# Strassen pairs of projections in the dilated part of an attention layer

## The chip, the cores and the metric

The kernel runs on one core of one Trainium2 chip, as one program. The metric is the device time of an execution in microseconds (us); lower is better. Times of before are the median of three runs, and a profile was taken of one more execution.

## The reference

The reference is an encoder trunk with two layers on 512 tokens of width 1024: h += Mixer(RMSNorm(h)), then h += SwiGLU(RMSNorm(h)). Layer 0 mixes by dilated sliding-window attention in three groups of 16 heads of 64, layer 1 by gated linear attention. The change lies in the first mixer:

```python
qkv = (h @ w_in).reshape(bsz, seq, A_N_GROUPS, 3, A_HEADS, A_HEAD_DIM)
for g, (window, dilation) in enumerate(((128, 1), (512, 4), (2048, 16))):
    q = rope(rms_norm(qkv[:, :, g, 0], q_gain[g]), positions)
    k = rope(rms_norm(qkv[:, :, g, 1], k_gain[g]), positions)
    v = qkv[:, :, g, 2]
    o, lse = dilated_window_attention(q, k, v, window, dilation)
...
alpha = softmax(stack(lses), axis=0)
out = sum(alpha[..., None] * stack(outs), axis=0)
return out.reshape(bsz, seq, A_WIDTH) @ w_out
```

## The kernel before

Everything is float32. A matrix product is made of three on TensorE (PE): both operands are split into a high and a low part, and hi·hi, hi·lo and lo·hi are added up in PSUM. A weight tile of 128 x 1024 comes by a DMA of 512 KB on the SP queue (`weight`), `split` copies it to the high part on ScalarE (ACT, L96) and subtracts that on VectorE (DVE, L97). There are two buffers for what is loaded (`wf`) and three each for the parts (`wh`, `wl`). The names in the profile are these tags: `wl<-wf,wh` is a low part being made.

The order of the instructions on each engine is laid down when the program is built, by a scheduler that goes by the order of the code and by priorities: loading and splitting stand under `high_priority(offset=AHEAD)` with AHEAD = 100, so they are drawn ahead of other work by so many places. Each engine then works through its own list strictly in order, waiting where an operand or a buffer isn't there.

The stages are: dilated attention (groups with dilations 4 and 16 together, 0 to about 414 us), local attention (to about 560), the output projection, the first FFN, the linear attention (about 950 to 1130), and the second FFN. The dilated part runs in four rounds u = 0 to 3 of four heads of either group. `attend_dilated` (L706) makes for each u a k chunk, a v chunk and a q chunk, and then attention. A chunk (`chunk_of`, L534) is a plain product of 512 tokens and 1024 features with 512 columns: 8 feature tiles x 4 token tiles x 3 = 96 matmuls of 128x512 (L548 to L550), four `pp` accumulators in PSUM (all that there are) and 4 weight tiles, each of which feeds 24 matmuls. Local attention begins with a chunk of the same size for its own q and k.

Behind a k or q chunk `qk_chunk` (L559) normalises and rotates: of each of four 128x512 tiles ACT copies the accumulator and squares it, DVE sums the squares by head (L573, L574), finds the reciprocal root (L116 to L119), multiplies by the tables of cosines and sines (L587, and in halves L588 and L589), adds (L590) and scales (L592). Then PE transposes in 16 blocks (L597) and the results are copied by ACT and DVE (L604, L606). All four tiles must be done before the first transpose. Attention computes scores on PE, softmax on DVE and ACT (L627, L628), transposes (L640), weighs v (L680), transposes back (L698) and stores by POOL's DMA queue (L719, L747).

The FFN's `gate_up` already uses seven products in place of eight, after Strassen: the inputs are cut into halves by features and tokens, the weights into halves by features and by the two columns that belong together, and sums of these are multiplied (`forms` L237 for weights, `product` L318 with L329 to L331). A product is 4 feature tiles x 2 token tiles x 3 = 24 matmuls and takes two split weight tiles, each feeding 12. Weight sums are made there by adding DMAs on POOL's queue (L252), 512 KB each, or on DVE.

The lines that the change and the prediction touch are in the functions below.

## Time and profile before

| | |
|---|---|
| time, median of three runs | 1509.53 us (1508.55 to 1509.82) |
| profiled execution, its own time | 1508.64 us |
| its span | 1506.8 us |
| PE busy | 1491.7 us, 99%, 8142 instructions |
| DVE busy | 947.9 us, 63% |
| ACT busy | 781.8 us, 52% |
| POOL busy | 110.3 us, 7% |
| HBM traffic | 121 GB/s over the span |

PE is the matrix engine; PEld, its weight loads, overlaps it. Busy time is the time in which an engine has an instruction running; consecutive instructions overlap, so a step is better read from start to start in a timeline. A row of a timeline has start and duration in us, the engine, the line in the kernel, the operation, out<-in by tile names without their numbers, and the shapes; brackets tell how long the engine had been idle before it and what ended that. A row of waits tells which instruction of which engine waited for what, and the total in us, the number and the longest. The row of a group has its instruction count, its busy time in us and the mean in ns, then the idle time in front of it.

### The profile page before, as it was taken

Reading aid. Unit: us, or ns where it says so; the run is one execution under the profiler, and the core shown is the slowest. Engines: PE = TensorE matmul, PEld = TensorE weight load, DVE = VectorE, ACT = ScalarE, POOL = GpSimd, SP = SyncE. Lnnn points to the kernel's source line nnn. Section 1 sums busy time; section 2 is a strip of 40 time slices with the busy share of each in tenths; the row PEclk is TensorE's granted clock in tenths of the full one; section 3 lists DMA queues with packets and bytes.
Section 4 is the critical chain, followed back from the end, with each engine's and each line's share of the span. In section 5 each row is a group of like instructions: output and inputs, shape, how many; then the busy total and the mean of one; then the engine's idle time right before and its main releaser. Section 6 shows DMA issues by size and latency. Waiting matters only on the chain.

```text
span 1506.8 us, 21145 instructions
## 1 busy us (share of the span) xinstructions
PE 1491.7 (99%) x8142; PEld 1225.9 (81%) x8142; DVE 947.9 (63%) x1728; ACT 781.8 (52%) x1348; POOL 110.3 (7%) x192
## 2 busy tenths in 40 slices
PE   8999999999999999999999999999999999999998
PEld 6878787887877878888888887888888888888887
DVE  6584766777476778866667334837476866668222
ACT  6353453545466655755567233545644855568121
POOL 0001010101010010211110000000010211110000
PEclk9999999999999999999999999999999999999999
DMA  8423222243222136777674333212156676675331
GB/s 281 158 67 94 81 79 84 85 128 99 74 71 71 44 121 194 224 168 156 148 162 129 92 100 96 91 56 78 46 157 188 195 170 153 156 152 147 118 110 60
DMA packets 59829, 183.95 MB, mean 122 GB/s; under 512 B 10032, under 2 KB 10608, under 8 KB 59728
## 3 DMA queue, kind: packets, MB, share of 16 engines
q1 hardware_dynamic: 44912, 133.17, 27.0%
q0 software_dynamic: 14816, 49.42, 16.4%
q8 instruction: 64, 1.05, 0.3%
q14 instruction: 37, 0.30, 0.1%
HBM read 174.11 MB, written 8.46 MB: 121 GB/s over the span
## 4 chain that ended last, share of the span: by engine, by line
PE 87%; DVE 8%; ACT 2%; DMA 1%; issue 1%; SPq 0%; ACTq 0%; DVEq 0%
PE ppp L109 9%; PE ppp L108 9%; PE ppp L110 9%; PE ppp L549 8%; PE ppp L550 8%; PE ppp L548 8%; PE ppp L329 6%; PE ppp L330 6%; PE ppp L331 6%; PE ps L331 2%; PE ps L329 2%; PE ps L330 2%; PE po L680 2%; PE ps L640 1%; DVE wl L97 1%
## 5 line engine op out<-in xcount | busy, mean ns | idle before, releaser
L97 DVE TENSOR_TENSOR wl<-wf,wh 128x1024 fp32r<-128x1024 f32 (+1 forms) x184 | 220.6, 1200 | 229.8 <-ACT wh L96 229.0
L96 ACT ACTIVATE wh<-wf 128x1024 fp32r<-128x1024 f32 (+1 forms) x184 | 191.3, 1040 | 326.7 <-PE ppp L109 195.2
L548 PE MATMUL ppp<-wh,xs 128*128 128x512 f32 (+1 forms) x672 | 256.7, 386 | 5.5 <-ACT wh L96 5.5
L549 PE MATMUL ppp<-wl,xs 128*128 128x512 f32 (+1 forms) x672 | 257.7, 383 | 0.7 <-DVE wl L97 0.3
L550 PE MATMUL ppp<-wh,xs 128*128 128x512 f32 (+1 forms) x672 | 257.5, 383 | 0.0
L548 PEld LDWEIGHTS ppp<-wh,xs 128*128 128x128 f32 x672 | 126.6, 189 | 32.4 <-ACT wh L96 5.5
L549 PEld LDWEIGHTS ppp<-wl,xs 128*128 128x128 f32 x672 | 126.8, 189 | 26.5 <-DVE wl L97 2.9
L550 PEld LDWEIGHTS ppp<-wh,xs 128*128 128x128 f32 x672 | 126.8, 189 | 25.0 <-issue 1.3
L97 DVE TENSOR_TENSOR wl<-wA,wh 128x1024 fp32r<-128x1024 f32 x88 | 107.6, 1222 | 37.8 <-ACT wh L96 37.8
L96 ACT ACTIVATE wh<-wA 128x1024 fp32r<-128x1024 f32 x88 | 93.2, 1059 | 62.1 <-PE ppp L331 45.8
L329 PE MATMUL ppp<-wh,a 128*128 128x512 f32 (+1 forms) x288 | 108.1, 381 | 0.0
L108 PE MATMUL ppp<-xs,wh 128*128 128x512 f32 x272 | 107.4, 396 | 0.0
L330 PE MATMUL ppp<-wl,a 128*128 128x512 f32 (+1 forms) x288 | 107.4, 373 | 0.0
L331 PE MATMUL ppp<-wh,a 128*128 128x512 f32 (+1 forms) x288 | 107.3, 374 | 0.0
L109 PE MATMUL ppp<-xs,wh 128*128 128x512 f32 x272 | 106.6, 393 | 0.0
L110 PE MATMUL ppp<-xs,wl 128*128 128x512 f32 x272 | 106.0, 391 | 0.0
L97 DVE TENSOR_TENSOR wl<-wB,wh 128x1024 fp32r<-128x1024 f32 x38 | 46.5, 1225 | 73.7 <-ACT wh L96 73.7
L628 ACT ACTIVATE sm<-sm,st 128x160 f32<-128x160 f32 (+2 forms) x128 | 56.8, 447 | 40.9 <-DVE st L627 40.8
L329 PE MATMUL ps<-wh,sh 128*128 128x512 f32 (+1 forms) x192 | 73.1, 381 | 0.0
L329 PE MATMUL ppp<-wh,sh 128*128 128x512 f32 (+1 forms) x192 | 72.2, 376 | 0.0
L331 PE MATMUL ppp<-wh,sl 128*128 128x512 f32 (+1 forms) x192 | 71.6, 373 | 0.0
L331 PE MATMUL ps<-wh,sl 128*128 128x512 f32 (+1 forms) x192 | 71.5, 373 | 0.0
(319 smaller groups left out, 2955.0 us busy)
## 6 DMA issues: line engine op xcount, KB each, us to landing
wA<-in_gate_up_dram POOLq DMA_DIRECT2D x52, 512.0 KB, 5.5
wf<-in_down_dram SPq DMA_DIRECT2D x32, 512.0 KB, 3.5
wf<-in_gate_up_dram SPq DMA_DIRECT2D x24, 512.0 KB, 4.5
wf<-in_a_w_v_dram SPq DMA_DIRECT2D x20, 512.0 KB, 3.4
wB<-in_gate_up_dram POOLq DMA_DIRECT2D x20, 512.0 KB, 5.5
wf<-in_a_w_q_dram SPq DMA_DIRECT2D x16, 512.0 KB, 3.3
wf<-in_a_w_qk_dram SPq DMA_DIRECT2D x16, 512.0 KB, 3.3
wB<-in_gate_up_dram SPq DMA_DIRECT2D x16, 512.0 KB, 3.3
```

Source lines behind the costliest of these rows:

```text
L96: nc.scalar.activation(hi, src, AF.Copy)
L97: self.low = nc.vector.tensor_sub(lo, src, hi.bitcast(F32))
L108: mm(out, lhsT=wh, rhs=xh, start=start, stop=False)
L109: mm(out, lhsT=wh, rhs=xl, start=False, stop=False)
L110: self.multiplied = mm(out, lhsT=wl, rhs=xh, start=False, stop=stop)
L329: mm(a, lhsT=xh[:, tok], rhs=wh[:, f], start=start and k == 0, stop=False, skip_group_check=True)
L330: mm(a, lhsT=xh[:, tok], rhs=wl[:, f], start=False, stop=False, skip_group_check=True)
L331: self.multiplied = mm(a, lhsT=xl[:, tok], rhs=wh[:, f], start=False, stop=k == last, skip_group_check=True)
L548: mm(a, lhsT=xh, rhs=wh[:, f], start=k == 0, stop=False)
L549: mm(a, lhsT=xh, rhs=wl[:, f], start=False, stop=False)
L550: self.multiplied = mm(a, lhsT=xl, rhs=wh[:, f], start=False, stop=k == KT - 1)
L628: nc.scalar.activation(sm[:, w], sm[:, w], AF.Exp, bias=n, scale=-1.0, accum_out=l)
```

## The change

The first k and the first q chunk stay plain. The other ten projections of the dilated part are made in five pairs, in this order: (v0,v1), (k1,q1), (k2,q2), (v2,v3), (k3,q3). A pair is one seven-product multiplication of halves: four halves of the input (by features and tokens), two projections side by side, 7 x 24 = 168 matmuls instead of 2 x 96 = 192.

- `input_sums` makes the four sums S1 to S4 of the input's halves, once, from the same rows that the plain chunk of k0 used. They lie in slots of the residual `h` and of other tiles that are free in this stage (`xs`, `h`, `R`, `acc`, `sq`, `fa`).
- `pair_forms` makes the seven forms of the weights: 8 plain loads on SP and 8 adding ones on POOL's queue, 512 KB each. Forms 3 and 5 are made in the tiles of forms 2 and 4: they are added to once those have been split. 14 tiles are split for a pair, instead of 8 for two chunks.
- `pair` multiplies in the order A11, S1, S2, S4, S3, A12, A22, on two pairs of `pp` accumulators in turn, and puts the results together: copies on ACT, four operations on DVE that read PSUM and add, and two additions. The second projection's four tiles are complete after the fifth product, the first one's after the seventh.
- The rotation is a function of its own, `rotated`, called first for q (the second of a pair) and then for k. Four small operations for the mean square are joined in one.
- Slots: `qk` 16 instead of 20, one of `qtmp` and `t2` instead of two; the tables for local attention are made at its start.

In after.py `split` is at L97 (ACT) and L98 (DVE), the plain chunk at L551 to L553, `product` at L330 to L332, and the operations of `rotated` at L585 to L616.

```diff
     BASE = {"xs": 16, "h": 8, "wf": 2, "wh": 3, "wl": 3, "R": 1, "acc": 1, "sq": 1,
             "cols": 1, "ident": 1, "ones": 1, "eps": 1}
-    ATTN = {"qk": 20, "v": 8, "zs": 4, "wa": 4, "wb": 2, "sm": 3, "pt": 4, "ob": 2, "on": 2, "ao": 4,
-            "tab": 2, "masks": 1, "ms": 1, "Rc": 1, "ebias": 1, "mst": 1,
-            "qv": 2, "qr": 2, "qtmp": 2, "st": 2, "t2": 2, "stn": 2, "st0": 2, "mw": 2, "mL": 5}
+    LOCAL = {"ao": 4, "on": 2, "tab": 2}
+    DILATED = {"zx": 4, "wA": 2, "wB": 2, "fa": 1}
+    ATTN = {"qk": 16, "v": 8, "zs": 4, "wa": 4, "wb": 2, "sm": 3, "pt": 4, "ob": 2, "masks": 1, "mRc": 1, "ms": 1, "Rc": 1, "ebias": 1, "mst": 1,
+            "qv": 2, "qr": 2, "qtmp": 1, "st": 2, "t2": 1, "stn": 2, "st0": 2, "mw": 2, "mL": 5}
...
+        self.tables({"k": ((1, 1), (1, 2)), "q": ((0, 1), (0, 2))}, 0, "pt", "qk")
...
+        return self.rotated(kind, rc, copy)
+
+    def rotated(self, kind, rc, source):
+        nc = self.nc
         zs = []
         v = self.t("qv", (P, 4, 8))
         for i in range(NT):
-            z = self.t("zs")
-            nc.scalar.activation(z, acc[i], AF.Copy)
+            z = source(i)
             sq = self.t("wb")
             nc.scalar.activation(sq, z, AF.Square)
             nc.vector.tensor_reduce(v[:, i], sq.rearrange("p (h d) -> p h d", d=HD), AX.X, ALU.add)
-            nc.vector.tensor_scalar(v[:, i], v[:, i], 1.0 / HD, self.ebias[:, rc + i:rc + i + 1],
-                                    op0=ALU.mult, op1=ALU.add)
             zs.append(z)
+        nc.vector.scalar_tensor_tensor(v, v, 1.0 / HD, self.ebias[:, rc:rc + 4].unsqueeze(2).to_broadcast([P, 4, 8]),
+                                       op0=ALU.mult, op1=ALU.add)
...
+    def split_tokens(self, k, i):
+        tok = slice(i % 2 * P, (i % 2 + 1) * P)
+        return [x[:, tok] for x in self.x[k][i // 2]]
+
+    def input_sums(self):
+        nc = self.nc
+        stt = nc.vector.scalar_tensor_tensor
+        half = KT // 2
+        minus = self.t("mst", (P, 4))
+        nc.vector.tensor_scalar(minus, self.cols[:, half:KT], -1.0, None, op0=ALU.mult)
+        tags = iter(["xs"] * 4 + ["h"] * 8 + ["R", "acc", "sq", "fa"])
+        out = []
+        for m in range(half):
+            lo = [self.t(next(tags), (P, 2, 256), F32R) for _ in range(2)]
+            hi = [self.t(next(tags), (P, 2, 256), F32R) for _ in range(2)]
+            raw = [self.t(tag, (P, 2, 256)) for tag in ("pt", "sm")]
+            f = [raw[i // 2][:, i % 2] for i in range(4)]
+            upper, lower = self.raw[m], self.raw[half + m]
+            nc.scalar.activation(raw[1], upper.rearrange("p (a b) -> p a b", b=256), AF.Copy,
+                                 scale=self.cols[:, m:m + 1])
+            stt(f[0], lower[:, 256:S], self.cols[:, half + m:half + m + 1], f[3], op0=ALU.mult, op1=ALU.subtract)
+            stt(f[1], f[0], -1.0, f[2], op0=ALU.mult, op1=ALU.subtract)
+            nc.vector.tensor_sub(f[2], f[2], f[3])
+            stt(f[3], lower[:, 0:256], minus[:, m:m + 1], f[1], op0=ALU.mult, op1=ALU.subtract)
+            for i in range(2):
+                nc.scalar.activation(hi[i], raw[i], AF.Copy)
+                nc.vector.tensor_sub(lo[i], raw[i], hi[i].bitcast(F32))
+            out.append([(hi[i // 2][:, i % 2], lo[i // 2][:, i % 2]) for i in range(4)])
+        self.raw = None
+        x = self.x
+        self.forms_of_x = [[x[m][0] for m in range(half)], [x[half + m][0] for m in range(half)],
+                           [x[half + m][1] for m in range(half)]] + [[out[m][i] for m in range(half)] for i in range(4)]
+
+    def pair_forms(self, first, second):
+        def load(tag, dram):
+            tiles = []
+            for i in range(2):
+                w = self.t(tag, (P, 1024))
+                self.nc.sync.dma_start(w, dram[i])
+                tiles.append(w)
+            return tiles
+
+        def add(tiles, dram):
+            for i in range(2):
+                self.nc.gpsimd.dma_start(tiles[i], dram[i], accum_op=ALU.add)
+
+        def ready(tiles):
+            return [self.split(w, (P, 1024), "wh", "wl") for w in tiles]
+
+        def steps():
+            a = load("wA", first[0:2])
+            add(a, second[0:2])
+            yield ready(load("wf", first[0:2]))
+            b = load("wB", second[2:4])
+            w = ready(a)
+            add(a, second[2:4])
+            yield w
+            yield ready(a)
+            add(a, first[2:4])
+            w = ready(b)
+            add(b, second[0:2])
+            yield w
+            yield ready(b)
+            yield ready(load("wf", first[2:4]))
+            yield ready(a)
+
+        gen = steps()
+        for _ in range(7):
+            with self.tc.high_priority(offset=AHEAD):
+                w = next(gen)
+            yield w
+
+    def pair(self, first, second, tile_of, scale):
+        nc = self.nc
+        A11, A12, A22, S1, S2, S3, S4 = self.forms_of_x
+        w = self.pair_forms(first, second)
+        b1 = [self.p("pp") for _ in range(2)]
+        b3 = [self.p("pp") for _ in range(2)]
+        out = [[None] * NT for _ in range(2)]
+
+        def copy(dst, src, c, i):
+            nc.scalar.activation(dst, src, AF.Copy, scale=scale(c, i))
+            return dst
+
+        self.product(b1, A11, next(w), S, True)
+        for i in range(2):
+            out[0][i] = copy(tile_of(0, i), b1[i], 0, i)
+        self.product(b3, S1, next(w), S, True)
+        for i in range(2):
+            out[1][2 + i] = copy(tile_of(1, 2 + i), b3[i], 1, 2 + i)
+        self.product(b1, S2, next(w), S, False)
+        for i in range(2):
+            out[1][i] = copy(tile_of(1, i), b1[i], 1, i)
+        self.product(b3, S4, next(w), S, False)
+        for i in range(2):
+            e = out[1][i]
+            nc.vector.scalar_tensor_tensor(e, b3[i], scale(1, i), e, op0=ALU.mult, op1=ALU.add)
+        self.product(b1, S3, next(w), S, False)
+        for i in range(2):
+            e = out[1][2 + i]
+            t = copy(self.t("zs"), b1[i], 1, 2 + i)
+            nc.vector.tensor_add(e, e, t)
+        yield out[1]
+        self.product(b3, A12, next(w), S, True)
+        for i in range(2):
+            e = out[0][i]
+            nc.vector.scalar_tensor_tensor(e, b3[i], scale(0, i), e, op0=ALU.mult, op1=ALU.add)
+        self.product(b1, A22, next(w), S, False)
+        for i in range(2):
+            out[0][2 + i] = copy(tile_of(0, 2 + i), b1[i], 0, 2 + i)
+        yield out[0]
+
+    def qk_pair(self, u):
+        early = lambda c, i: self.t("zx" if (c == 0) == (i < 2) else "zs")
+        sums = self.pair(self.ins["a_w_k"][u], self.ins["a_w_q"][u], early, lambda c, i: (1.0, -1.0)[c])
+        z = next(sums)
+        q = self.rotated("q", 0, lambda i: z[i])
+        z = next(sums)
+        k = self.rotated("k", 0, lambda i: z[i])
+        return k, q
+
+    def v_pair(self, u):
+        scale = lambda c, i: (self.Rc, self.minus_Rc)[c][:, i:i + 1]
+        sums = self.pair(self.ins["a_w_v"][u], self.ins["a_w_v"][u + 1], lambda c, i: self.t("v"), scale)
+        second, first = next(sums), next(sums)
+        return first, second
 
     def attention(self):
         self.masks = None
         self.pending = None
         self.later = []
         with self.phase("attn", self.ATTN):
-            self.ready = self.first_tiles()
-            far = [self.attend_dilated(u) for u in range(4)]
+            far = []
+            with self.phase("dilated", self.DILATED):
+                self.ready = self.first_tiles()
+                k = self.qk_chunk("k", 0)
+                self.input_sums()
+                q = self.qk_chunk("q", 0)
+                v = self.v_pair(0)
+                far.append(self.attend_dilated(0, k, v[0], q))
+                k, q = self.qk_pair(1)
+                far.append(self.attend_dilated(1, k, v[1], q))
+                k, q = self.qk_pair(2)
+                v = self.v_pair(2)
+                far.append(self.attend_dilated(2, k, v[0], q))
+                k, q = self.qk_pair(3)
+                far.append(self.attend_dilated(3, k, v[1], q))
+                self.forms_of_x = None
```

How this moves instructions. First PE, at the end of u=1's last projection (q in before; k and q together now). `wh` and `wl` are a weight tile's parts, `xs` the input's, `ppp` the accumulators, `wa` a rotated tile. Before:

```order
L548 MATMUL ppp_1377<-wh_1470,xs_166 128x512
L549 MATMUL ppp_1377<-wl_1471,xs_166 128x512
L550 MATMUL ppp_1377<-wh_1470,xs_167 128x512
L548 MATMUL ppp_1847<-wh_1853,xs_82 128x512
L549 MATMUL ppp_1847<-wl_1854,xs_82 128x512
L550 MATMUL ppp_1847<-wh_1853,xs_83 128x512
...
L549 MATMUL ppp_1847<-wl_1914,xs_142 128x512
L550 MATMUL ppp_1847<-wh_1913,xs_143 128x512
L597 MATMUL ps_1559<-ident_65,wa_1552 128x128
```

After:

```order
L330 MATMUL ppp_1237<-wh_1560,xs_177 128x512
L331 MATMUL ppp_1237<-wl_1561,xs_177 128x512
L332 MATMUL ppp_1237<-wh_1560,xs_178 128x512
L330 MATMUL ppp_1930<-wh_1944,xs_85 128x512
L330 MATMUL ppp_1931<-wh_1944,xs_85 128x512
L330 MATMUL ppp_1932<-wh_1984,xs_452 128x512
L330 MATMUL ppp_1933<-wh_1984,xs_452 128x512
L609 MATMUL ps_1490<-ident_65,wa_1483 128x128
...
L331 MATMUL ppp_1930<-wl_1945,xs_85 128x512
L330 MATMUL ppp_1930<-wh_1944,xs_99 128x512
L609 MATMUL ps_1642<-ident_65,wa_1635 128x128
```

Before, 63 matmuls of the next chunk stand between the last one of the projection and the first transpose of q (`wa_1552`). Now it is 4 matmuls to the first transpose of q (`wa_1483`), then q's 16 transposes, then 5 more matmuls to the first of k (`wa_1635`); the first of those five reads `wl_1945`, and the others stand behind it.

Now DVE at the same place; `wb` and `wa` are the rotation's tiles, `qr` the reciprocal roots, `wl` the low part of a weight tile. Before:

```order
L97 TENSOR_TENSOR wl_1471<-wf_1468,wh_1470 128x1024
L97 TENSOR_TENSOR wl_1854<-wf_1851,wh_1853 128x1024
L97 TENSOR_TENSOR wl_1884<-wf_1881,wh_1883 128x1024
L587 TENSOR_TENSOR wa_1531<-zs_1499,qk_290 128x512
...
L592 TENSOR_TENSOR wa_1545<-wa_1545,qr_1523 128x512
L589 TENSOR_TENSOR wb_1553<-zs_1517,qk_293 128x8x32
L97 TENSOR_TENSOR wl_1914<-wf_1911,wh_1913 128x1024
L590 TENSOR_TENSOR wa_1552<-wa_1552,wb_1553 128x512
L97 TENSOR_TENSOR wl_1944<-wf_1941,wh_1943 128x1024
L592 TENSOR_TENSOR wa_1552<-wa_1552,qr_1523 128x512
L604 COPY qk_1571<-ps_1566 128x512
```

After:

```order
L98 TENSOR_TENSOR wl_1561<-wA_1242,wh_1560 128x1024
...
L600 TENSOR_TENSOR wb_1636<-zs_1590,qk_296 128x8x32
L604 TENSOR_TENSOR wa_1628<-wa_1628,qr_1606 128x512
L601 TENSOR_TENSOR wb_1636<-zs_1590,qk_296 128x8x32
L98 TENSOR_TENSOR wl_1945<-wf_1940,wh_1944 128x1024
L602 TENSOR_TENSOR wa_1635<-wa_1635,wb_1636 128x512
L98 TENSOR_TENSOR wl_1949<-wf_1942,wh_1948 128x1024
L604 TENSOR_TENSOR wa_1635<-wa_1635,qr_1606 128x512
L98 TENSOR_TENSOR wl_1985<-wA_1934,wh_1984 128x1024
L616 COPY qk_1654<-ps_1649 128x512
```

Before, two tiles of the next chunk (`wl_1854`, `wl_1884`) are split ahead of q's rotation, and two more within it. Now no tile of the next pair is split between the last one of the pair (`wl_1561`) and nearly the end of k's rotation: all that remains of q's rotation and most of k's stands ahead of `wl_1945`, the next pair's first.

78 lines of the change are left out of this document (49 added, 29 removed).

## The prediction

> **What bounds the kernel now.** I read the busy table of the page first, then the busy time by stretch, then the timelines of PE and DVE, then waits and transfers.
>
> ```profile
> PE 1491.7 (99%) x8142; PEld 1225.9 (81%) x8142; DVE 947.9 (63%) x1728; ACT 781.8 (52%) x1348; POOL 110.3 (7%) x192
> ```
>
> PE is busy 99% of the span, so on the page every matmul taken out is time saved. The stretches that the change touches are the four rounds of dilated attention, 0 to about 414 us. Two whole rounds, and last a stretch of the FFN that runs as seven products already (columns: stretch, length, busy us and instructions of PE, PEld, DVE, ACT, POOL, then granted clock, DMA share, GB/s):
>
> ```profile
> 81.50:164.70 83.20, 83.07 (x556) 66.78 (x555) 54.51 (x141) 37.07 (x82) 4.91 (x9) 1.00 0.25 80
> 164.70:247.90 83.20, 83.08 (x570) 67.05 (x569) 53.14 (x137) 37.81 (x84) 6.69 (x13) 1.00 0.27 83
> 639.60:682.20 42.60, 42.60 (x197) 34.99 (x196) 27.77 (x30) 25.59 (x33) 5.10 (x6) 1.00 0.66 148
> ```
>
> PE has no gap in a round, while DVE is busy 54.51 of 83.20 us (66%). A round is four things for DVE: splitting weights, normalising and rotating k, the same for q, and softmax. Its steps, from the rotation of the last q projection (start, duration, engine, line, operation):
>
> ```profile
> 322.05 0.68 DVE L587 TENSOR_TENSOR wa<-zs,qk 128x512 f32<-128x512 f32 x1
> 322.65 0.68 DVE L573 TENSOR_REDUCE qv<-wb 128x8 f32<-128x512 f32 x1
> 323.25 0.68 DVE L587 TENSOR_TENSOR wa<-zs,qk 128x512 f32<-128x512 f32 x1
> ...
> 328.04 0.42 DVE L588 TENSOR_TENSOR wb<-zs,qk 128x256 f32<-128x256 f32 x1
> 328.37 0.42 DVE L589 TENSOR_TENSOR wb<-zs,qk 128x256 f32<-128x256 f32 x1
> 328.71 0.18 DVE L116 TENSOR_TENSOR qtmp<-qr 128x32 f32<-128x32 f32 x1
> 328.81 0.42 DVE L588 TENSOR_TENSOR wb<-zs,qk 128x256 f32<-128x256 f32 x1
> ...
> 334.06 1.22 DVE L97 TENSOR_TENSOR wl<-wf,wh 128x1024 fp32r<-128x1024 f32 x1
> 335.19 0.68 DVE L590 TENSOR_TENSOR wa<-wa,wb 128x512 f32<-128x512 f32 x1
> 335.80 1.22 DVE L97 TENSOR_TENSOR wl<-wf,wh 128x1024 fp32r<-128x1024 f32 x1
> 336.93 0.68 DVE L592 TENSOR_TENSOR wa<-wa,qr 128x512 f32<-128x512 f32 x1
> 337.53 0.81 DVE L139 SCALAR_TENSOR_TENSOR xs<-on,cols,xs 128x576 fp32r<-128x576 f32 x1
> ```
>
> Durations overlap, so I count from start to start: 0.60 us for an operation on 128x512 (322.05, 322.65, 323.25), 0.33 for a half multiplication (328.04 to 328.37), 0.10 for a small one (328.71 to 328.81), 1.13 for a weight split (334.06 to 335.19). From 322.05 to 337.53 are 15.5 us with two splits in them: 13.2 us for the rotation of one projection. In before this is free: behind a k or q projection PE has another plain chunk, and the order lists 63 of its matmuls ahead of the transposes. That cover is what I follow.
>
> **Part 1, the matmuls.** By the order, each of the three lines of the plain chunks goes from 672 to 352 matmuls and each of the seven products' from 672 to 952: 3 x (320 - 280) = 120 matmuls of 128x512 fewer. Their step:
>
> ```profile
> 83.62 0.39 PE L548 MATMUL ppp<-wh,xs 128*128 128x512 f32 x1
> 83.85 0.39 PE L549 MATMUL ppp<-wl,xs 128*128 128x512 f32 x1
> 84.08 0.39 PE L550 MATMUL ppp<-wh,xs 128*128 128x512 f32 x1
> 84.31 0.39 PE L548 MATMUL ppp<-wh,xs 128*128 128x512 f32 x1
> ```
>
> 0.69 us for three, 0.227 each: 120 x 0.227 = 27.2 us less, since PE is the bound without gap. That is the ceiling of the gain, because nothing else is removed from PE. A product of 24 matmuls is 5.44 us, a seven-product pair 38.1 us.
>
> **Part 2, what DVE gets.** A pair splits 14 weight tiles where two chunks split 8: 6 x 1.13 = 6.8 us. Four reads of PSUM with an addition and two additions are 6 x 0.60 = 3.6 us. So about 10.4 us more for a pair, less 0.1 or 0.4 us for joined small operations. A round of before has DVE 54.5 and PE 83.2 us. A period that holds one k,q pair and one attention has 14 splits where a round of before has 12, so DVE needs 54.5 + 2 x 1.13 + 3.6 = 60.4 us; PE needs 83.2 less three chunks of 96 x 0.227 = 21.8, which leaves 17.8, and 38.1 of products: 55.9 us. There DVE is the longer one, so what counts is where its work stands in order. How long a split takes on DVE and, ahead of it, on ACT:
>
> ```profile
> L97 DVE TENSOR_TENSOR wl<-wA,wh 128x1024 fp32r<-128x1024 f32 x88 | 107.6, 1222 | 37.8 <-ACT wh L96 37.8
> L96 ACT ACTIVATE wh<-wA 128x1024 fp32r<-128x1024 f32 x88 | 93.2, 1059 | 62.1 <-PE ppp L331 45.8
> ```
>
> *Boundary of the k1,q1 pair and the next pair.* Let T0 be the end of the pair's seventh product. The three weight buffers are let go one in 2.72 us (12 matmuls); the last split of the pair can't start before the middle of product 6 (T0-8.2) and its two steps take 1.06 + 1.22 us, so it ends between T0-5.9 and T0-2.7, when PE needs it; I take T0-4.5. Behind it stand in DVE's order, for q: 1 reduction, 8 half multiplications, 1 multiplication, 4 additions, 4 scalings, 2 PSUM reads of 128x512 and 5 small ones: 12 x 0.60 + 8 x 0.33 + 0.5 = 10.4 us. So q's transposes start at T0+5.9. Then k, the whole: 4 reductions, 2 copies, 4 multiplications, 8 halves, 3 additions, 3 scalings, 5 small: 16 x 0.60 + 8 x 0.33 + 0.5 = 12.7, and only then the next pair's first split, 1.13: T0+19.7. k's transposes wait for two more 128x512 operations and one split, T0+22.1. Eight transposes stand 0.88 us apart from the next four, 0.11 each; the first scores follow a copy:
>
> ```profile
> 337.98 1.03 PE L597 MATMUL ps<-ident,wa 128*128 128x128 f32 x8
> 338.86 0.60 PE L597 MATMUL pt<-ident,wa 128*128 128x128 f32 x4
> ```
>
> Up to k's transposes PE has 9 matmuls (2.0) and q's 16 transposes (1.8). Of the 22.1 us 18.3 are idle, and about 1.3 more pass from k's transposes through the copies (0.6, two of them on DVE) to the scores: about 20 (17 to 22, by the place of the last split).
>
> *Boundary of the k3,q3 pair and local attention.* The same 10.4 for q, then k with three splits among its operations: 4 reductions, 2 copies, 4 multiplications, 4 additions, 4 scalings, 8 halves, 5 small and 3 x 1.13 = 17.3. k's transposes at T0+23.2; PE has 8 matmuls and 16 transposes (3.6): about 21 with the copies (17 to 25).
>
> *Boundary of the k2,q2 pair and the v pair.* The first split here stands earlier, behind 9.3 us of q's operations: T0+4.8, idle 4.3. But the k rotation then stands among the v pair's splits: 22 us (six splits and 12.7 + 2 x 0.60 + 1.3) up to the fourth product's first, at T0+27, where PE arrives at T0+22.9 (4.8, three products of 5.44 and 16 transposes): 4.1 more; with 1.5 for its additions about 10 (5 to 14).
>
> *First round.* k's rotation and a split, 13.8 us, stand ahead of q's later splits, and two tiles in hand feed 24 matmuls each, 10.9 us: 2.9 late. The same again with q's rotation in the v pair, and one addition on the way, about 1: I take 7 (3 to 10).
>
> At nothing: the sums of input halves on DVE, four times 5 half and 2 whole operations, 4 x (1.7 + 1.2) = 11.4 us, lie beside the plain q chunk (21.8 us of PE); without that cover they would be part of the 10. The local tables are four operations of half size, and 16 slots for q and k instead of 20 hold one round and half of the next, whose transposes come only when the round's scores are long done.
>
> **Part 3, the adding loads.** 16 x 512 KB a pair, half of them by POOL's queue. Their time to landing, the wait they make in before, and the one that is on the chain of before:
>
> ```profile
> wA<-in_gate_up_dram POOLq DMA_DIRECT2D x52, 512.0 KB, 5.5
> wf<-in_a_w_v_dram SPq DMA_DIRECT2D x20, 512.0 KB, 3.4
> ACT wh L96 <- DMA wB<-in_gate_up_dram: 28.3, 16, 3.2
> 771.88 5.32 DMA wB<-in_gate_up_dram
> 1341.66 5.65 DMA wB<-in_gate_up_dram
> ```
>
> Two forms of a pair (the third and the fifth) are made by adding to tiles that the form ahead still has to split, so they can start only when those splits are done: 5.5 us against 5.44 us of the product between plus what the buffers lead. In before 16 waits took 28.3 us of ACT and are on the chain twice, once in each FFN. Over ten such places I take 3.5 (0 to 10). The plain loads and POOL's issuing lie beside PE's work: the DMA share is 0.25 in these rounds and 0.66 in the gapless FFN stretch; without that cover it would be the 5.5 of each.
>
> **Part 4, the clock after idle time.** The first matmuls of before, after 5.47 us of idle:
>
> ```profile
> 5.47 0.80 PE L548 MATMUL ppp<-wh,xs 128*128 128x512 f32 x1 [5.47 <-ACT wh L96]
> ...
> 7.29 0.63 PE L548 MATMUL ppp<-wh,xs 128*128 128x512 f32 x1
> 7.71 0.63 PE L549 MATMUL ppp<-wl,xs 128*128 128x512 f32 x1
> 8.14 0.63 PE L550 MATMUL ppp<-wh,xs 128*128 128x512 f32 x1
> 8.57 0.63 PE L548 MATMUL ppp<-wh,xs 128*128 128x512 f32 x1
> 8.99 0.47 PE L549 MATMUL ppp<-wl,xs 128*128 128x512 f32 x1
> 9.30 0.39 PE L550 MATMUL ppp<-wh,xs 128*128 128x512 f32 x1
> 9.53 0.40 PE L548 MATMUL ppp<-wh,xs 128*128 128x512 f32 x1
> ```
>
> The step is 0.43 us until 8.99 and 0.23 after: eight steps by 0.2 are 1.6 us lost, though the clock column shows 1.00. With three or four idle stretches of over 5 us in the boundaries above I take 5 us (0, if the start alone is slow, to 8). The Trainium skill, "TensorE: Matmul & The Clock Gate", Part 1, says that the array falls to half rate after an idle window of about 3.4 us and stays so for about 3.4 us of work; the row agrees in size, and an estimate by the skill's page would be 1.7 us lost for each such stretch, which speaks against a change that opens idle stretches.
>
> **Sum.** 20 + 21 + 10 + 7 + 3.5 + 5 = 66.5, less 27.2: 39.3 us slower. The profiled execution has 1508.64 us of its own with a span of 1506.8; the median of the runs is 1509.53, 0.9 above. 1508.64 + 39.3 + 0.9 = 1548.8, so 1549. The low ends (17 + 17 + 5 + 3 + 0 + 0 = 42) give 1509.5 + 14.8 = 1524, the high ends (22 + 25 + 14 + 10 + 10 + 8 = 89) 1509.5 + 61.8 = 1571.
>
> **Rivals.** *Faster: the rotations stay hidden.* If DVE's operations run ahead of the order's look (q's rotation begins already behind product 4, and its reductions in product 6), the boundaries cost only a few us. It decides once all stalls together are under 27.2 us. For it: the FFN stretch above, seven products with additions and no gap in PE. Against it: there DVE has 0.65 us of work for one of PE, here 60.4 for 55.9, and 9 matmuls stand ahead of k's transposes instead of 63. All stalls together would be 0 to 8: 1482 to 1490, about 1486. Chance 0.09. The Trainium skill, "Perfetto Trace Analysis", Identifying the Most-Contended Engine, says to optimize the busiest engine first; by that rule this cut of PE would pay in full, and it leaves out that the engine behind it takes the bound over.
>
> *Slower still: each added form is late.* If the adding loads are not led by the buffers, each of the ten places costs about the 5.3 us that the exposed one at 771.88 took on the chain: 10 x 5.3 = 53 instead of 3.5, 1509.5 + 39.3 + 49.5, about 1598. It decides from the point where a load takes longer than the 5.44 us product that covers it. Against it: of the 16 waits in the FFNs, two are on the chain. Chance 0.05.
>
> *Break-even.* Both boundaries of 20 us shrink to about 5 each, the third stays at 10 and all the rest is 7: stalls of 27, and 1509 again, 1506 to 1512. Chance 0.03. That the change doesn't do what it says is excluded by the order's counts. The rest, 0.83, is the forecast.
>
> **Numbers.** A measurement of this kernel tells 0.2% (3 us) from no change. Faster comes from the first rival, 0.09; the same from the break-even, 0.03; slower from the forecast and the late forms, 0.88. The range is the forecast's own, 1524 to 1571, which leaves out the three rivals (0.17) and holds the time 8 times in 10.
>
> **What would show it.** Right: in the profile after, PE idle of 12 us and more in one piece twice (before local attention and after the k1,q1 pair), each ended by DVE with L98 or the transposes' L604; DVE above 85% in these rounds; PE's total busy time 27 us lower plus the cold starts. Wrong: PE without gaps over 4 us at the ends of the pairs, or gaps ended by a transfer. If DVE's rows show the next pair's first split ahead of the k rotation, part 2 is wrong in its place.

## The result and the profile after

The changed kernel takes 1577.71 us (median of four runs, 1576.75 to 1582.42), the kernel before 1509.04 beside it: a ratio of 1.0461, 95% interval 1.0439 to 1.0483, 68.7 us slower. The forecast was 1549, range 1524 to 1571. The profiled execution is the longest of the four, 1582.42 us with a span of 1580.3, so its rows hold some 5 us more than the median.

The busy table of the changed kernel, and the row of granted clock in 40 slices of 39.5 us:

```profile
PE 1500.9 (95%) x8022; PEld 1226.3 (78%) x8022; DVE 1011.3 (64%) x1782; ACT 827.9 (52%) x1404; POOL 145.7 (9%) x232
PEclk9989799996899999999999999999999999999999
```

Two differences to before lie in these lines. PE has 120 instructions less, yet is busy 9.2 us longer (1500.9 for 1491.7): the 27.2 us that were taken out are there, so 36.4 us of busy time came in. And PE's idle time is 79.4 us (1580.3 less 1500.9) for 15.1 before: 64.3 more. 64.3 + 36.4 - 27.2 = 73.5, the difference of the two spans. The clock row has a 6, a 7 and two 8s in the first eleven slices, where before had none below 9.

The stretches of the rounds, in the windows used for before (stretch, length, busy us and instructions of PE, PEld, DVE, ACT, POOL, granted clock, DMA share, GB/s):

```profile
81.50:164.70 83.20, 77.07 (x494) 61.11 (x493) 49.13 (x106) 44.32 (x84) 12.60 (x18) 0.91 0.67 155
164.70:247.90 83.20, 66.39 (x455) 51.19 (x453) 59.69 (x141) 40.01 (x85) 13.83 (x21) 0.86 0.49 108
247.90:331.30 83.40, 69.17 (x475) 54.81 (x476) 58.84 (x124) 41.73 (x84) 12.71 (x17) 0.92 0.68 148
331.30:414.50 83.20, 63.31 (x433) 49.58 (x435) 57.67 (x131) 37.69 (x76) 8.65 (x16) 0.82 0.40 110
```

PE is no longer without gaps, and no other engine is busy throughout either: DVE is at 59 to 72%. All three engines wait for each other in turn. Where PE waits is seen in its timeline; these are its instructions with idle time ahead of them (in brackets: how long, and what ended it):

```profile
45.34 0.54 PE L552 MATMUL ppp<-wl,xs 128*128 128x512 f32 x1 [2.97 <-DVE wl L98]
78.50 0.50 PE L331 MATMUL ppp<-wl,xs 128*128 128x512 f32 x1 [2.42 <-DVE wl L98]
111.89 1.12 PE L652 MATMUL ps<-ident,sm 128*128 128x128 f32 x4 [4.54 <-ACT sm L640]
149.43 0.50 PE L330 MATMUL ppp<-wh,h 128*128 128x512 f32 x1 [0.84 <-ACT wh L97]
150.69 0.50 PE L331 MATMUL ppp<-wl,h 128*128 128x512 f32 x1 [0.76 <-DVE wl L98]
169.89 0.76 PE L330 MATMUL ppp<-wh,xs 128*128 128x512 f32 x1 [2.73 <-DVE zx L966]
187.04 0.79 PE L331 MATMUL ppp<-wl,xs 128*128 128x512 f32 x1 [11.71 <-DVE wl L98]
253.20 0.79 PE L330 MATMUL ppp<-wh,xs 128*128 128x512 f32 x1 [5.76 <-ACT zs L941]
280.61 0.80 PE L331 MATMUL ppp<-wl,xs 128*128 128x512 f32 x1 [5.73 <-DVE wl L98]
312.64 0.66 PE L652 MATMUL ps<-ident,sm 128*128 128x128 f32 x4 [1.98 <-ACT sm L640]
370.63 1.94 PE L609 MATMUL ps<-ident,wa 128*128 128x128 f32 x8 [7.36 <-DVE wa L604]
381.34 0.80 PE L551 MATMUL ppp<-wh,xs 128*128 128x512 f32 x1 [7.46 <-ACT xs L139]
388.05 1.94 PE L609 MATMUL ps<-ident,wa 128*128 128x128 f32 x8 [2.92 <-DVE wa L604]
426.60 0.50 PE L551 MATMUL ppp<-wh,xs 128*128 128x512 f32 x1 [2.25 <-ACT xs L139]
```

The k1,q1 pair ends at 165.8 (T0), the k3,q3 pair at 363.1. Around them are 15.0 us of idle time (2.73, 11.71 and two short ones) and 20.0 (the last four rows), around the end of the k2,q2 pair 11.5 (253.20 and 280.61). The first round has 5.4 (45.34, 78.50). The rest, 11.9 us, stands at splits of added tiles, and of the tiles next to them, and at softmax (111.89, 149.43, 150.69, 312.64, and pieces of 0.6 to 1.0 us at 231.95, 233.21, 314.95, 348.37 and 349.63). Together 63.8 of the 64.3.

DVE at the first of these ends, up to the split that PE's row at 187.04 waits for:

```profile
184.83 0.69 DVE L604 TENSOR_TENSOR wa<-wa,qr 128x512 f32<-128x512 f32 x1
185.43 0.42 DVE L601 TENSOR_TENSOR wb<-zs,qk 128x256 f32<-128x256 f32 x1
185.77 1.22 DVE L98 TENSOR_TENSOR wl<-wf,wh 128x1024 fp32r<-128x1024 f32 x1
```

DVE pauses for 1.4 us in all from 157 to 189: q's rotation, then k's, then the split, as its order said.

The half rate shows in the steps behind idle time. Behind the two short pieces at 149 and 150 us:

```profile
150.69 0.50 PE L331 MATMUL ppp<-wl,h 128*128 128x512 f32 x1 [0.76 <-DVE wl L98]
...
151.50 0.63 PE L331 MATMUL ppp<-wl,h 128*128 128x512 f32 x1
151.92 0.63 PE L332 MATMUL ppp<-wh,h 128*128 128x512 f32 x1
152.35 0.63 PE L330 MATMUL ppp<-wh,fa 128*128 128x512 f32 x1
...
154.48 0.58 PE L332 MATMUL ppp<-wh,acc 128*128 128x512 f32 x1
154.90 0.39 PE L330 MATMUL ppp<-wh,xs 128*128 128x512 f32 x1
155.13 0.39 PE L331 MATMUL ppp<-wl,xs 128*128 128x512 f32 x1
```

The step is 0.43 us from 151.50 to 154.48 and 0.23 after. The eight transposes at 370.63 last 1.94 us, where eight lasted 1.03 before. Counting each instruction from its start to the next one's, or to its own end where idle time follows, the 36.4 us divide like this: the 128x512 matmuls hold 24.4 (4.1 of it where idle time follows, since there are 17 more such places and an instruction in front of a gap is shown busy beyond its step), the 128x128 transposes 8.5 and the smaller matmuls 3.6.

The trace's record of the granted clock has two values, 1.00 and 0.50. In the changed kernel it is at 0.50 in twelve stretches, the longest of 23.9 us, 92.2 us in all; before, in none from 9.1 us to the end of its work. PE is busy for 63.5 of the 92.2 us, and about half of that, 32 us, is what half rate costs.

### The profile page after: what moved, and what is told of

Same layout as the page of the kernel before. It is cut to its first block, busy times and chain, and to the rows that moved or that the text cites. A ratio compares the mean times of both kernels' runs of the same rounds, so it can differ in the third digit from the quotient of the medians.

```text
span 1580.3 us, 21151 instructions
## 1 busy us (share of the span) xinstructions
PE 1500.9 (95%) x8022; PEld 1226.3 (78%) x8022; DVE 1011.3 (64%) x1782; ACT 827.9 (52%) x1404; POOL 145.7 (9%) x232
## 3 DMA queue, kind: packets, MB, share of 16 engines
q8 instruction: 63, 1.03, 0.3%
## 4 chain that ended last, share of the span: by engine, by line
PE 76%; DVE 12%; DMA 6%; ACT 3%; issue 2%; SPq 0%; ACTq 0%; POOLq 0%; DVEq 0%
PE ppp L110 8%; PE ppp L109 8%; PE ppp L111 8%; PE ppp L331 8%; PE ppp L332 8%; PE ppp L330 8%; PE ppp L553 3%; PE ppp L552 3%; PE ppp L551 3%; DVE wl L98 3%; PE ps L332 2%; PE ps L330 2%; PE ps L331 2%; PE po L692 2%; PE ps L652 1%
## 5 line engine op out<-in xcount | busy, mean ns | idle before, releaser
L97 ACT ACTIVATE wh<-wf 128x1024 fp32r<-128x1024 f32 (+1 forms) x164 | 170.0, 1037 | 276.3 <-PE ppp L110 190.2
L98 DVE TENSOR_TENSOR wl<-wf,wh 128x1024 fp32r<-128x1024 f32 (+1 forms) x164 | 196.1, 1197 | 170.7 <-ACT wh L97 170.6
L98 DVE TENSOR_TENSOR wl<-wA,wh 128x1024 fp32r<-128x1024 f32 x118 | 144.3, 1223 | 60.3 <-ACT wh L97 60.0
L97 ACT ACTIVATE wh<-wA 128x1024 fp32r<-128x1024 f32 x118 | 124.9, 1059 | 97.5 <-PE ppp L332 57.3
L98 DVE TENSOR_TENSOR wl<-wB,wh 128x1024 fp32r<-128x1024 f32 x58 | 71.0, 1225 | 113.9 <-ACT wh L97 108.8
L551 PE MATMUL ppp<-wh,xs 128*128 128x512 f32 (+1 forms) x336 | 128.0, 383 | 15.3 <-ACT xs L139 9.7
L552 PE MATMUL ppp<-wl,xs 128*128 128x512 f32 (+1 forms) x336 | 128.6, 383 | 3.0 <-DVE wl L98 3.0
L553 PE MATMUL ppp<-wh,xs 128*128 128x512 f32 (+1 forms) x336 | 127.7, 384 | 0.0
L330 PE MATMUL ppp<-wh,a 128*128 128x512 f32 (+1 forms) x288 | 108.2, 381 | 0.0
L332 PE MATMUL ppp<-wh,a 128*128 128x512 f32 (+1 forms) x288 | 107.3, 374 | 0.0
L97 ACT ACTIVATE wh<-wB 128x1024 fp32r<-128x1024 f32 x58 | 61.5, 1060 | 71.2 <-DMA wB<-in_gate_up_dram 27.9
L551 PEld LDWEIGHTS ppp<-wh,xs 128*128 128x128 f32 x336 | 65.0, 193 | 29.4 <-ACT xs L139 10.4
L331 PE MATMUL ppp<-wl,xs 128*128 128x512 f32 x160 | 67.0, 419 | 20.7 <-DVE wl L98 20.7
L552 PEld LDWEIGHTS ppp<-wl,xs 128*128 128x128 f32 x336 | 65.5, 195 | 15.6 <-DVE wl L98 3.8
L330 PE MATMUL ppp<-wh,xs 128*128 128x512 f32 x160 | 66.4, 417 | 9.0 <-ACT zs L941 5.9
L553 PEld LDWEIGHTS ppp<-wh,xs 128*128 128x128 f32 x336 | 64.8, 194 | 12.2 <-issue 1.1
L330 PE MATMUL ps<-wh,sh 128*128 128x512 f32 (+1 forms) x192 | 73.1, 381 | 0.0
```

The costliest lines, as they stand in the source:

```text
L97: nc.scalar.activation(hi, src, AF.Copy)
L98: self.low = nc.vector.tensor_sub(lo, src, hi.bitcast(F32))
L330: mm(a, lhsT=xh[:, tok], rhs=wh[:, f], start=start and k == 0, stop=False, skip_group_check=True)
L331: mm(a, lhsT=xh[:, tok], rhs=wl[:, f], start=False, stop=False, skip_group_check=True)
L332: self.multiplied = mm(a, lhsT=xl[:, tok], rhs=wh[:, f], start=False, stop=k == last, skip_group_check=True)
L551: mm(a, lhsT=xh, rhs=wh[:, f], start=k == 0, stop=False)
```

## The experiments

Theory A was the prediction's: DVE has the rotations ahead of the next splits, PE idles, and idle time halves its rate for a while. Theory B: the adding loads come late and make the stalls. Theory C: the clock is low for a reason other than idle time. Every kernel was timed beside the kernel before, whose median was 1508.67 to 1509.52. Four of them (the two with plain loads on SP's queue, plain loads on GpSimd's queue, no second additions) leave weight sums out, so they tell of time alone: what they compute isn't the reference.

| kernel | us | ratio, 95% interval |
|---|---|---|
| the changed kernel | 1577.71 | 1.0439 to 1.0483 |
| offset 200 | 1576.03 | 1.0410 to 1.0486 |
| plain loads for adding ones | 1547.03 | 1.0241 to 1.0275 |
| v pairs only | 1531.12 | 1.0124 to 1.0155 |
| idle time filled | 1569.47 | 1.0375 to 1.0406 |
| offset 400 | 1559.91 | 1.0317 to 1.0356 |
| offset 400, plain loads | 1533.70 | 1.0134 to 1.0180 |
| offset 400, early local input | 1546.74 | 1.0226 to 1.0259 |
| v pairs only, offset 400 | 1535.64 | 1.0162 to 1.0192 |
| sums on GpSimd | 1589.39 | 1.0514 to 1.0547 |
| all together, sums on GpSimd | 1568.34 | 1.0368 to 1.0402 |
| plain loads on GpSimd's queue | 1557.73 | 1.0292 to 1.0360 |
| no second additions | 1556.86 | 1.0284 to 1.0326 |

**The order on DVE.** First the priority offset of a pair's forms was doubled:

```diff
-            with self.tc.high_priority(offset=AHEAD):
+            with self.tc.high_priority(offset=2 * AHEAD):
                 w = next(gen)
```

> The weight forms of a pair get twice the priority offset (200 for 100), nothing else. Theory A (the rotations of q and k stand on VectorE ahead of the next pair's splits; PE idles there, and each idle stretch is followed by matmuls at half rate): the idle at the ends of the k1,q1 and the k2,q2 pair goes, 26 us and about 10 us of slow matmuls with it, the end of the k3,q3 pair stays: about 1540 us, granted clock 0.98 to 0.99. Theory B (the adding loads come late and make the stalls): 1570 us or more, since the loads are the same. Theory C (the clock is lower for another reason than idle time, the seven products or the traffic themselves): idle goes but the clock stays 0.97, about 1555 us.

1576.03, no difference, and the idle piece at the end of the k1,q1 pair was still 11.70 us. This run didn't test what it was meant to: at 200 the splits stood behind both rotations still, as DVE's timeline showed. The same edit with `4 * AHEAD`:

> As the first try at the order, with the offset of a pair's weight forms at 400: only now does the listing of VectorE have the next pair's splits spread through the rotations of q and k (at 200 they stood behind both still, so that run told nothing of this place). Theory A (the rotations ahead of the splits are a cause of their own): the idle of 14 us at the end of the k1,q1 pair and of 11 us at the end of the k2,q2 pair goes and some 8 us of half-rate matmuls with it: about 1543 us. Theory B (it is the adding loads alone, through the queue of ScalarE and VectorE behind a split that waits for one): 1570 to 1580, the idle moves to the splits of added tiles.

1559.91, 17.8 us less, between the two theories' times. PE's waits in this kernel (what waited for what, us in all, times, longest):

```profile
PE ppp L551 <- ACT wh L97: 14.7, 2, 9.2
PE ps L609 <- DVE wa L604: 11.3, 3, 7.3
PE ppp L551 <- ACT xs L139: 9.7, 2, 7.3
PE ppp L330 <- ACT wh L97: 4.2, 4, 1.2
```

The wait for a low part of 11.7 us is gone: at the end of the k1,q1 pair 1.8 + 1.8 us are left of 15.0 (with 2.9 and 1.2 further on that are new), and about 4 of the 11.5 at the next pair. The end before local attention is unchanged (7.33, 7.33, 2.66, 2.36), since its splits have other priorities, and the first round got new ones, the longest 9.2 us ahead of q's chunk, where it waits for its own weights. So the order is a cause of its own, and theory A holds for these two places; 17.8 us is what is left of its worth after those new waits.

**The adding loads.**

```diff
-                self.nc.gpsimd.dma_start(tiles[i], dram[i], accum_op=ALU.add)
+                self.nc.sync.dma_start(tiles[i], dram[i])
```

> The adding loads on GpSimd's queue are made plain loads of the same size on SP's queue into the same tiles (the weight sums are left out, so the products are not those of the reference). Theory A: the stalls at the ends of the pairs stay, 0 to 10 us less than the changed kernel, 1567 to 1578. Theory B: most of the loss goes, about 1520.

1547.03, 30.7 us less, while A gave at most 10 and B nearly 60. Neither was right: the adding loads are a second cause, worth nearly half of the loss. Its busy table:

```profile
PE 1483.9 (96%) x8022; PEld 1217.3 (79%) x8022; DVE 1010.1 (65%) x1782; ACT 828.1 (54%) x1404; POOL 110.2 (7%) x192
```

With offset 400 as well:

> Offset 400 and plain loads in place of the adding ones together (the weight sums are left out). Theory A: the two causes are apart and add up: 1547 less some 30, about 1517. Theory B: no better than the plain loads alone, 1545.

1533.70. The loads are worth 26.2 us there and 30.7 without the offset, the order 13.3 with plain loads and 17.8 with adding ones: two causes that nearly add up. Without both the kernel is still 24.2 us slower than before: of 48.5 us of idle time in its profile, 19.2 stand before local attention and 8.5 ahead of q's first chunk. How the loads work is seen in ScalarE's timeline of the changed kernel, ahead of PE's wait at 111.89:

```profile
102.91 1.37 ACT L941 ACTIVATE v<-ppp,Rc 128x512 f32<-128x512 f32 x2 [0.98 <-PE ppp L332]
109.14 1.06 ACT L97 ACTIVATE wh<-wA 128x1024 fp32r<-128x1024 f32 x1 [4.86 <-DMA wA<-in_a_w_q_dram]
110.10 0.41 ACT L640 ACTIVATE sm<-sm,st 128x160 f32<-128x160 f32 x1
```

The high part of a tile waits 4.86 us for its addition to land, and softmax's exponentials, which need nothing of it, stand behind it in ScalarE's queue. PE's transposes at 111.89 wait for those. The 4.54 us of that row, and all but a little of the 11.9 us at such places, are gone in the run with plain loads.

Which property of the loads it is, two more runs asked. One kept them on GpSimd's queue without adding (`self.nc.gpsimd.dma_start(tiles[i], dram[i])`):

> The adding loads stay on GpSimd's queue and at their places, but load instead of adding (the weight sums are left out). Theory A (it is the longer landing of an adding load, 5.5 us and more against 3.4): 1550 to 1555, near the run with plain loads on SP's queue (1547). Theory B (it is the queue: GpSimd issues late, behind stores and waits): 1570 or more.

1557.73, 20.0 us less than adding. The median time to landing of the k weights that are added to `wA`, in the changed kernel and in this one:

```profile
wA<-in_a_w_k_dram POOLq DMA_DIRECT2D x6, 512.0 KB, 5.5
```

```profile
wA<-in_a_w_k_dram POOLq DMA_DIRECT2D x6, 512.0 KB, 3.5
```

So about two thirds go with the adding and a third with GpSimd's queue in the place of SP's. The five groups of these loads in the dilated part land 1.4 to 3.8 us later (medians) when they add; that the later landing is what costs, and nothing else about adding, is argued from the waits. The other run left out the additions that make forms 3 and 5, loads and all:

```diff
-            w = ready(a)
-            add(a, second[2:4])
-            yield w
+            yield ready(a)
...
-            w = ready(b)
-            add(b, second[0:2])
-            yield w
+            yield ready(b)
```

> Only the additions that make forms 3 and 5 in the tiles of forms 2 and 4 are left out (4 of a pair's 8 adding loads, those tiles are split as they are). Theory A (these back-to-back places are where an addition can't be early enough, as the prediction had it): most of the 30 us goes, 1550 or less. Theory B (any adding load costs): about half, 1562.

1556.86 (one of its four executions took 5177.91 us, for which nothing here shows a cause; the other three have a median of 1556.00, 21.7 less than the changed kernel). Leaving out this half of the adding loads, those whose sum is the very next form, saves 21.7 us, where making all of them plain saves 30.7. It takes 2 MB of transfers out of each pair as well, so the two can't be set against each other exactly.

**The clock.** Spare matmuls in the place of idle time, which write a PSUM tile that k's transposes overwrite:

```diff
+            if c == 0 and warm:
+                with self.tc.issue_after(behind()):
+                    for _ in range(warm):
+                        nc.tensor.matmul(ps, lhsT=self.spare[:, 0:P], rhs=self.spare, start=True, stop=True)
             lead = turn(NT - 1)
...
-        k = self.rotated("k", 0, lambda i: z[i])
+        k = self.rotated("k", 0, lambda i: z[i], {1: 46, 3: 60}.get(u, 0), lambda: self.turned_last.ins)
```

> Spare matmuls of 128x512 that nothing reads stand on PE between q's and k's transposes at the ends of the k1,q1 pair (46) and the k3,q3 pair (60), where the changed kernel idles about 12 and 10 us. Theory A: the matmuls and transposes behind run at the full step at once, 5 to 9 us less than the changed kernel, about 1570, and granted clock 0.98. Theory C: the same time as the changed kernel or more, 1577 to 1582, clock 0.97.

1569.47, 8.2 us less, within A's 5 to 9, and nothing that C allows. The time at a clock of 0.50 falls from 92.2 us to 44.4. Behind the fill (the row of 46) the steps are whole:

```profile
172.02 11.16 PE L613 MATMUL ps<-xs 128*128 128x512 f32 x46
184.08 0.50 PE L331 MATMUL ppp<-wl,xs 128*128 128x512 f32 x1 [0.90 <-DVE wl L98]
184.42 0.39 PE L332 MATMUL ppp<-wh,xs 128*128 128x512 f32 x1
184.65 0.39 PE L331 MATMUL ppp<-wl,xs 128*128 128x512 f32 x1
...
186.73 1.03 PE L609 MATMUL ps<-ident,wa 128*128 128x128 f32 x8
```

In the changed kernel the same matmuls, behind 11.71 us of idle time, went in steps of 0.43:

```profile
187.63 0.63 PE L332 MATMUL ppp<-wh,xs 128*128 128x512 f32 x1
188.06 0.63 PE L331 MATMUL ppp<-wl,xs 128*128 128x512 f32 x1
188.49 0.63 PE L332 MATMUL ppp<-wh,xs 128*128 128x512 f32 x1
```

Only two of the stalls were filled. How much idle time it takes is read from the clock's record, which changes in steps of 3.41 us. Three pairs of neighbouring steps of the changed kernel (stretch, length, PE's busy us and instructions, granted clock, DMA share, GB/s):

```profile
148.06:151.47 3.41, 1.81 (x7) 1.00 0.04 13
151.47:154.88 3.41, 3.41 (x9) 0.50 0.76 217
346.03:349.44 3.41, 1.83 (x7) 1.00 0.29 85
349.44:352.86 3.42, 3.23 (x14) 1.00 0.00 0
192.43:195.84 3.41, 3.41 (x46) 1.00 0.96 156
195.84:199.26 3.42, 3.42 (x10) 0.50 0.03 5
```

With 1.60 us of idle time in a step the next one is at half rate, with 1.58 it is not. The 14 profiles of this case have 6048 steps at full rate with another behind them. The clock fell to 0.50 right after all 86 steps that hold over 1.91 us of PE's idle time, after 13 of the 28 with 1.48 to 1.91, and after 6 of the 5934 with less. So it is the idle time within one step that counts, and short pieces add up. The six are another matter, and one of them is in the last pair above: PE has no gap there, but at least 2.47 us of the step are score matmuls of 64 rows (`ps<-qk,qk`); no step with less of those fell without idle time. So theory C has a share: one of the twelve falls of the changed kernel, and three steps that stayed at 0.50 without idle time (from 113.92, 390.40 and 393.82). Why the border is blurred between 1.48 and 1.91 us, these runs don't show.

**Parts alone.** The v pairs only, with k and q as plain chunks (`qk_chunk` in the place of `qk_pair`):

> Only the two v pairs stay seven products; k and q are plain chunks. 48 matmuls of 128x512 fewer than before, 10.9 us. Theory A: no rotation stands between two pairs except behind q chunks that run 21.8 us each: 1500 to 1510. Theory B: ten late loads become four, 1509 - 11 + 4 x 5 = about 1518 and PE waits for transfers.

1531.12, above both. 10.9 us are gone from PE, and its profiled span is still 21.9 us longer than before. Its idle time is 33 us for 15: 5.1 of what came in stand in the first round, 3.1 at the second v pair, 5.51 and 0.94 before local attention, and 4.07 at softmax. That last one stands not behind an added tile but behind one of k's that came by a plain load: ScalarE waited 4.39 us for it, with the exponentials behind. The rest is half rate and the gaps' edges. The chunks before local attention are plain in this run, so what is lost there, about 9 of the 21.9 us with the half rate behind it (an estimate from the gaps and the clock's record), can't come from a k,q pair. Other parts of the change, the slots or the place of local attention's tables and input, may be the cause; no run took those alone. So the change loses even without a k,q pair, but it isn't shown that the products alone do it. With offset 400 for all weights of the part:

> Only the two v pairs as seven products, all weights of the dilated part at offset 400. Theory A: the first round's idle in the q chunk goes (3 us), the rest stays with the adding loads: about 1523 us against 1531. Theory B: 1528 to 1531.

1535.64, rather worse: the waits moved. 2.8 us in the first round became 2.3, 2.7 more stand ahead of the first matmul, and two new ones of 2.3 and 4.1 us came at transposes.

**Before local attention.** Offset 400, for the plain weights of this part too, and

```diff
+            with self.tc.high_priority(offset=4 * AHEAD):
+                self.load_x("xT", 64)
             self.tables({"qk": ((0, 0), (1, 0))}, 1, "on", "tab")
-            self.load_x("xT", 64)
```

> Offset 400 for the forms, also for the plain weights of the first round, and for the loads and splits of local attention's input, whose tables come after. If the idle before local attention (18 us) comes from the input tiles that are made behind the rotations: 10 to 15 us under the run with offset 400 alone. If it comes from the rotation itself or from slots that the last product frees: the same within 4 us.

1546.74, 13.2 less than offset 400 alone. Not all of it is local attention's: the idle time there fell by about 4.5 us (5.33, 6.33, 2.44 and 1.06 for 7.33, 7.33, 2.66 and 2.36), and the 9.2 us in the first round became 2.4 with 3.2 more ahead of the first matmul.

**Sums without adding loads.** A plain load into a spare tile and an addition on GpSimd:

```diff
-            for i in range(2):
-                self.nc.gpsimd.dma_start(tiles[i], dram[i], accum_op=ALU.add)
+            for i, w in enumerate(load("wf", dram)):
+                self.nc.gpsimd.tensor_add(tiles[i], tiles[i], w)
```

> Each adding load becomes a plain load on SP's queue into a spare tile and an addition of 128x1024 on GpSimd itself, everything else as in the changed kernel. What is tested: is it the time from the release of a tile to the landing of the addition (about 6 us) that costs the 30 us which the plain loads saved, or something else about them, such as the sums themselves? Theory A (the time from release to landing): if GpSimd adds in 2 to 3 us, about 1550 to 1560; Theory B (GpSimd is slower than the load, 6 us and more, or it slows VectorE down): 1577 or more.

1589.39, slower than the changed kernel by 11.7. The addition itself is quick enough, but DVE is held up by it: the additions, and DVE's splits of the same tiles (least, median and most ns), read

```profile
L904 POOL TENSOR_TENSOR wA<-wA,wf 128x1024 f32<-128x1024 f32 x30 | 82.8, 2760 | 208.4 <-DVE wl L98 87.4 <-DMA wf<-in_a_w_v_dram 46.7 <-DMA wA<-in_a_w_k_dram 34.3
L98 DVE TENSOR_TENSOR wl<-wA,wh x118: 1209/1219/3203, 61.3 to 1458.0; 128x1024 fp32r<-128x1024 f32 x118
```

2.76 us, as A had it, but a split beside one takes up to 3.2 us for 1.22, and DVE is busy 1046 us for 1011. Of the 14 splits of weights in the dilated part that overlap an addition, five took 1.21 to 1.22 us, and the other nine 1.08 to 1.09 us beyond the time that they shared with it: as if they stood still until the addition was done. Two other things differ in this run and are not separated from that: ScalarE's high parts waited 30.6 us for sums on GpSimd (six times, at most 12.5), and SP's next loads waited until GpSimd let go of the tiles that it adds. So the run doesn't tell whether the later landing alone makes an adding load dear. With offset 400 and the early local input:

> The sums on GpSimd together with offset 400 and the early input of local attention: what the runs point to as the best version with seven products. From 1547 less the 20 to 26 us that the loads cost there: about 1522; 1547 or more if GpSimd's additions are slow. Below 1509 only if the idle before local attention went as well, which nothing here does.

1568.34, 21.6 more than the same with adding loads. No version tried beats the kernel before; the best that computes the whole is the v pairs alone at 1531.12, and of those with all five pairs 1546.74.

## Why the prediction was wrong

The direction and the mechanism at the pairs' ends were right; the size was not. Step by step, from the two profiled executions:

| term | forecast | measured |
|---|---|---|
| 120 matmuls | -27.2 | 8142 to 8022 instructions; the accounts close with -27.2 |
| end of the k1,q1 pair | 20 | 15.0 idle |
| end of the k3,q3 pair | 21 | 20.0 idle |
| end of the k2,q2 pair | 10 | 11.5 idle |
| first round | 7 | 5.4 idle |
| late additions | 3.5 (0 to 10) | 11.9 idle; 30.7 in time when replaced, half rate included |
| half rate after idle time | 5 (0 to 8) | about 32 by the clock's record; 36.4 of busy time came in |

- **The places.** Counted from the instruction order and DVE's steps, q's transposes at the first end were to start at T0+5.9 and k's at T0+22.1; they started at T0+5.9 (171.69) and T0+23.7 (189.47). At the last end it was T0+7.5 and T0+24.9 for 5.9 and 23.2. Working from an order of instructions with steps from a trace came within 2 us here. The first rival, rotations that stay hidden, is out.
- **The step that failed most: the clock, part 4.** It took 5 us where the profile has 36.4 of added busy time, about 32 of it half rate: 31.4 too little. The idle terms came to 63.8 us for 61.5. That is 33.7 us in all; less the 4.7 us by which the profiled execution is longer than the median it is 29.0, and the forecast missed the median by 28.9. "With three or four idle stretches of over 5 us" took only long stalls, at 1.6 us each. There were twelve stretches at half rate, 2.6 us lost in each on average, because the rate fell behind as little as 1.6 us of idle time in a step of 3.41 us, and then stayed low through all 90 steps of the 14 profiles that were at 0.50 and held 1 us or more of idle time. The Trainium skill, "TensorE: Matmul & The Clock Gate", Part 1, names an idle window of about 3.4 us ahead of the half rate; at 150 us two pieces of 0.84 and 0.76 us were enough.
- **Luck in the idle terms.** That they came within 2.3 us in sum is partly luck: the ends of the pairs and the first round had 6.1 us less than forecast, the late additions 8.4 more.
- **The other one: the adding loads.** "Of the 16 waits in the FFNs, two are on the chain" was carried over from a stage without softmax. In the FFNs of before PE has no gap over 0.65 us, so nothing that it needed at once stood behind a split that waited. Here softmax does, in ScalarE's queue and in DVE's. The places meant have 11.9 us of idle time for 3.5, just over the end of 10. In the run without additions idle time fell by more, 20.9 us (58.5 for 79.4, part of it at the pairs' ends), and PE's busy time by 17.0 (1483.9 for 1500.9): the late loads bring half rate and gap edges too, 30.7 us by the medians.
- **The signs named.** "PE idle of 12 us and more in one piece twice" was not met. The longest piece was 11.71 us, ended by L98 as named. Before local attention there were four, the longest 7.46, and two of them (7.46 and 2.25) waited for local attention's input tiles from ScalarE (`xs`, L139), which the forecast left out; k's transposes came late enough behind them that the sum still fits. DVE was not above 85% in these rounds but at 59 to 72%, though it was the one that PE waited for: it waits itself, for ScalarE's high parts and for PE's transposes. "PE's total busy time 27 us lower plus the cold starts" was right in form, and was the line that gave the clock term away. The second rival, ten places at 5.3 us, put 53 us where leaving these additions out saved 21.7.

What stays open: what adding costs beyond the later landing, what the slots and the moved tables of local attention cost by themselves, and what the two v pairs lose beyond the rows named.

## What to carry to other kernels

Price a stall of PE as its length plus what comes behind it, and count the short ones, two close together as one: here 64 us of idle time brought another 36 of busy time, about 32 of it half rate. Work that was free behind a long plain product isn't free behind one that is cut into pieces with operands to prepare: ask for every engine's queue what stands behind the first instruction that can wait, and whether PE needs it. And when a change takes work from PE but gives some to three others, hold the expected gain (27 us) against what the order does at each seam, since one round with PE at 99% tells nothing of the next engine's queue.

## What was not expected of the hardware

Half rate came behind 3.41 us steps with only 1.6 us of idle time, in two pieces, and in six places of the 14 profiles behind steps of small score matmuls without any. An adding load of 512 KB landed after 5.5 us where a plain one on the same queue took 3.5. GpSimd's additions of 128x1024 in SBUF took 2.76 us, and DVE's splits beside them up to 3.2 us instead of 1.22; the Trainium skill, "GPSIMD Engine Reference", Specifications, says that GpSimd shares its SBUF interfaces with VectorE where that reads two SBUF inputs, and these splits do.
